# Preparing summed weight tiles in a fixed, lagged order, with the plain copies on ScalarE's DMA queue

## The chip, the cores and the metric

The kernel runs on one core of a Trainium2 chip. Its time is the device time of one execution in microseconds (us); lower is better. The engines are TensorE (PE in the profile, its weight loads PEld), VectorE (DVE), ScalarE (ACT), GpSimd (POOL) and SyncE (SP), each with a queue of its own that it works through in order, and 16 DMA engines that move the data. SP, ScalarE and GpSimd start transfers. A transfer that adds to what is in memory is called an accumulate here; all of them are on GpSimd's queue.

## The reference

A transformer trunk of two layers on 512 tokens of width 1024, in float32. Each layer is an FFN, a mixer with three kinds of attention, and a second FFN:

```
for l in range(DEPTH):
    h = rms_norm(x, norm_g[l, 0])
    x = x + 0.5 * swiglu(h, ffn_w_gate[l, 0], ffn_w_up[l, 0], ffn_w_down[l, 0])
    h = rms_norm(x, norm_g[l, 1])
    ...
    x = x + merged @ w_o[l]
    h = rms_norm(x, norm_g[l, 2])
    x = x + 0.5 * swiglu(h, ffn_w_gate[l, 1], ffn_w_up[l, 1], ffn_w_down[l, 1])
return rms_norm(x, final_g)
```

with `swiglu(h, w_gate, w_up, w_down) = (silu(h @ w_gate) * (h @ w_up)) @ w_down`. The hidden width of the FFN is 2816, 22 tiles of 128. The mixer's branches are neighbourhood attention, differential attention and windowed attention with grouped keys.

## The kernel before

Every product is made of float32 parts: a weight tile is loaded by SP (`weights`, line 90), rounded by ScalarE to its high part (`whi`, line 91), VectorE takes the rest (`wlo`, line 92), and TensorE adds three products (lines 113 to 116). `weights` is called 74 times in a mixer and 24 times in an FFN's down projection (8 output tiles, three pieces each).

The gate and up products of an FFN run for most tiles in class `Seven`: a gate and an up tile of weights form a 2x2 block matrix, and seven products of sums of blocks do the work of eight. For that, sums of weight blocks are needed. In the first FFN they are made as it runs. For the three later FFNs, named (0, 1), (1, 0) and (1, 1) by layer and half, they are prepared ahead in DRAM by `prepare(l, i)`, while earlier work runs. For each of 20 tiles (k = 2 to 21) there are five transfers:

- `d_odd` (line 465): half of the gate and half of the up tile are copied to DRAM by SP's queue; `d_even` (line 466): the gate tile likewise. 512 KB each.
- Three accumulates on GpSimd's queue, all from line 456: the up tile onto `d_odd` (512 KB), half of `d_odd` onto half of `d_even` (256 KB), half of `d_even` onto its other half (256 KB). The second needs the first and both copies, the third needs the second.

`prepare` is a generator. Its step k issues the copies of tile k, the first accumulate of tile k - 2, the second of tile k - 4 and the third of tile k - 6; 26 steps do an FFN. `ahead_by(n)` adds n to what is owed and takes a step for each whole one: `weights` calls it with PACE["mixer"] or PACE["down"], `Seven.tile` with PACE["seven"]. `drained` takes what is left of an FFN's steps before that FFN starts.

What a step issues isn't what stands in the queues: a scheduler orders the instructions of each engine by when it takes their inputs to be ready. `tc.issue_after(loaded[0])` puts what SP issues in a step behind the weight load just issued; nothing fixes the place of the accumulates. Inside `Seven.tile` the method `in_order` chains the instructions of each engine in the order written.

Also on GpSimd's queue stand: the loads `x` and `lg` of the residual (line 62) and its stores `d_x` (line 67); the reciprocal root of a norm (`rs`) and of the differential attention's norm (`rt`), line 177, which TensorE spreads by transposes on line 184; the exchanges `qks` (lines 905, 906); and in neighbourhood attention the bias `nab` (line 1081) and the clearing of `lg` (line 1109), which TensorE transposes on line 1042. The lines 113 to 116, 368 to 371 (down projection), 555 (`Seven`) and 1052 (attention) are TensorE's.

Of the kernel before, what the change touches and what calls it, by code (L numbers as in the profile page):

```python
# [14 lines left out]
ALU = mybir.AluOpType  # L15

P = 128
S = 512
# [11 lines left out]
NA_WIN = (0, 64, 192, 256)  # L30
T5_STEPS = (8, 12, 16, 23, 32, 46, 64, 91)
GBUFS = 2 * MF
PACE = {"mixer": (0.36, 0.3), "seven": {(0, 1): 0.4}, "down": {(0, 0): 0.3, (0, 1): 0.4, (1, 0): 0.25}}
LOW_FIRST = (2, 4, 7)
WIDE, WIDE_FIRST = frozenset((2, 3, 4, 5, 6, 7)), frozenset((3, 4, 5))

# [2 lines left out]
def encoder(ctx: ExitStack, tc: tile.TileContext, a: dict, out: bass.AP):  # L39
# [3 lines left out]
    nc = tc.nc  # L43
# [35 lines left out]


    loaded, lower = [], []
    prepared, ahead, due, owed = {}, [], [], [0.0, 0.0]

    def weights(src, width=1024):
        raw = wpool.tile([P, 1024], F32, tag="raw", name="raw", bufs=3)
        hi = wpool.tile([P, 1024], F32R, tag="whi", name="whi")
        lo = wpool.tile([P, 1024], F32R, tag="wlo", name="wlo")
        for c in range(0, src.shape[-1], width):
            w = slice(c, min(c + width, src.shape[-1]))
            loaded[:] = [nc.sync.dma_start(raw[:, w], src[:, w]).ins]  # L90
            nc.scalar.copy(hi[:, w], raw[:, w])  # L91
            lower[:] = [nc.vector.tensor_tensor(out=lo[:, w], in0=raw[:, w], in1=f(hi[:, w]), op=ALU.subtract).ins]  # L92
        ahead_by(owed[1])
        return hi, lo
# [185 lines left out]
    def ffn(l, i, h, nxt=None):  # L280

        with tc.tile_pool(name="ffn", bufs=1) as fp, ExitStack() as order:
# [71 lines left out]
            if nxt is None:  # L354
                finish(fp, ghi, glo, h, tiles)
                return
            owed[1] = PACE["down"].get((l, i), 0)
            for m in range(KC):
# [87 lines left out]
    def prepare(l, i):  # L446


        prepared[l, i] = {}
        tiles = prepared[l, i]  # L450

        def flat(t):
            return t.rearrange("p n c -> p (n c)")

        def accumulate(out, more):
            nc.gpsimd.dma_start(out, more, accum_op=ALU.add, max_dma_last_dim=4 * 1024)  # L456

        for k in range(2, MF + 6):
            if k < MF:
                gu = a["w_gu"][l, i, k]  # L460
                t31, t24 = [
                    dram.tile([P, 2, S], F32, tag=f"d_{g}{l}{i}_{k}", name=f"d_{g}") for g in ("odd", "even")
                ]
                tiles[k] = t31, t24
                nc.sync.dma_start(t31, gu.rearrange("n p c -> p n c")[:, :, 0:S])
                nc.sync.dma_start(flat(t24), gu[0])
            if k - 2 in tiles:
                accumulate(flat(tiles[k - 2][0]), a["w_gu"][l, i, k - 2, 1])
            if k - 4 in tiles:
                t31, t24 = tiles[k - 4]  # L470
                accumulate(t24[:, 0], t31[:, 1])
            if k - 6 in tiles:
                t24 = tiles[k - 6][1]
                accumulate(t24[:, 1], t24[:, 0])
            yield

    def ahead_by(n):

        owed[0] += n
        while ahead and owed[0] >= 1:  # L480
            owed[0] -= 1
            with tc.issue_after(loaded[0]):
                if next(ahead[0], ahead) is ahead:
                    ahead.pop(0)
                    due.pop(0)

    def drained(l, i):

# [5 lines left out]
    class Seven:  # L494
# [9 lines left out]
        @contextmanager  # L504
        def in_order(self):


            traced = nc.cur_bb.bb.instructions
            last = traced[-1]
            yield  # L510
            start = next(k for k in reversed(range(len(traced))) if traced[k] is last) + 1
            for ins in traced[start:]:
                if ins.engine in self.behind:
                    why = mybir.DependencyInfo(mybir.DependencyClass.NoSync, mybir.DependencyReason.DATA)
                    tc.add_manual_dep(ins, self.behind[ins.engine].name, why, reason="in_order")
                self.behind[ins.engine] = ins

        def fetch(self, m, sums=None):
# [67 lines left out]
        def tile(self, m):  # L586
# [10 lines left out]
            def blocks(w, at=0):  # L597
                return [[t[:, at + k * P : at + k * P + P] for k in range(4)] for t in w]
# [4 lines left out]
            def side(n):  # L603
                return [s.t[n - 1] for s in sides]
# [17 lines left out]
            with self.in_order():  # L622
# [48 lines left out]
                nc.vector.tensor_tensor(out=gn, in0=gn, in1=h.rb, op=ALU.mult)  # L671
                self.product(7, one, blocks(w31), side(3))
            ahead_by(PACE["seven"].get(self.at, 0))
            u3 = self.halves(1, 6, 7)
            hi = fp.tile([P, S], F32R, tag="g", name="g", bufs=GBUFS)
# [702 lines left out]
    def gain(l, i):  # L1378
        return ng[:, (l * 3 + i) * KC : (l * 3 + i + 1) * KC]

    h = Norm(0, gain(0, 0))
    due[:] = [(0, 1), (1, 0), (1, 1)]
    ahead[:] = [prepare(*at) for at in due]
    for l in range(DEPTH):
        n1 = Norm(3 * l + 1, gain(l, 1))
        ffn(l, 0, h, n1)
        n2 = Norm(3 * l + 2, gain(l, 2))
        owed[1] = PACE["mixer"][l]
        mixer(l, n1, n2)
# [94 lines left out]
```

## Time and profile before

| | us |
|---|---|
| median of 3 runs | 2521.67 |
| lowest, highest | 2518.4, 2543.03 |
| the profiled execution, whole | 2516.38 |
| its span, first to last instruction | 2514.5 |
| TensorE idle within the span | 100.6 (2514.5 - 2413.9) |
| mean granted TensorE clock | 0.982 |

The first FFN ends at about 343 us, mixer 0 at 886, the second FFN at 1262, the third at 1618, mixer 1 at 2140. A busy time is that of one engine in the whole span or in a stretch; a wait is time in which an engine stood idle, put down to what released it. The granted clock is the share of its full speed that TensorE was given.

### The profile page before, as it was taken

To read this page: it belongs to the slowest core of one execution; us is meant where nothing else is said; L and a number is where in the kernel's file an instruction comes from. 1 tells how busy PE (TensorE), PEld (TensorE's weight loads), DVE (VectorE), ACT (ScalarE), POOL (GpSimd) and SP (SyncE) were. 2 spreads that over 40 slices of the span, in tenths; PEclk is the share of its full clock that TensorE was granted. 3 is DMA by queue.
4 is the path that set the end of the run, shared out by engine and by line. 5 is a ranking of instruction groups with operands and counts; after the bars stand their busy time and mean duration, and the time that the engine had idled before them with its cause. 6 is when DMAs were issued, how large, how long until landed. Compare 5 with 4: busy or idle time off the path is not lost. (4 is left out here: it accounts for less than half of the span.)

```text
span 2514.5 us, 34878 instructions
## 1 busy us (share of the span) xinstructions
PE 2413.9 (96%) x12762; PEld 2063.4 (82%) x12762; DVE 1722.1 (68%) x3061; ACT 1328.3 (53%) x2433; POOL 349.0 (14%) x524
## 2 busy tenths in 40 slices
PE   9999997898999999999899999988999999999998
PEld 7899876787888888888788888767888888888887
DVE  7998334675766678995379983345667667799932
ACT  6565224664666546663246662246655665566632
POOL 2100213322100011111200002133221000000000
PEclk9999998999999999999999999989999999999999
DMA  6566898676325559899645568866766323455532
GB/s 199 164 182 203 226 276 186 166 202 170 94 89 150 181 178 287 271 276 267 168 157 185 193 200 236 234 166 151 206 171 164 98 84 121 152 196 185 184 115 71
DMA packets 149771, 452.86 MB, mean 180 GB/s; under 512 B 18264, under 2 KB 23688, under 8 KB 148640
## 3 DMA queue, kind: packets, MB, share of 16 engines
q1 hardware_dynamic: 108096, 341.42, 40.1%
q0 software_dynamic: 40352, 107.36, 21.6%
q8 instruction: 100, 1.64, 0.3%
q10 hardware_dynamic: 1152, 1.86, 0.2%
q14 instruction: 71, 0.58, 0.1%
HBM read 428.52 MB, written 138.44 MB: 225 GB/s over the span
## 5 line engine op out<-in xcount | busy, mean ns | idle before, releaser
L91 ACT CAST whi<-raw 128x1024 fp32r<-128x1024 f32 (+1 forms) x258 | 264.6, 1031 | 397.7 <-PE mm L369 149.2
L92 DVE TENSOR_TENSOR wlo<-raw,whi 128x1024 fp32r<-128x1024 f32 (+1 forms) x258 | 321.2, 1246 | 214.5 <-ACT whi L91 120.2
L113 PE MATMUL mm<-h,whi 128*128 128x512 f32 x800 | 321.6, 402 | 0.7 <-ACT h L144 0.7
L114 PE MATMUL mm<-h,whi 128*128 128x512 f32 x800 | 316.2, 395 | 0.0
L368 PE MATMUL mm<-g,whi 128*128 128x512 f32 x528 | 208.0, 394 | 7.5 <-ACT whi L91 7.5
L369 PE MATMUL mm<-g,whi 128*128 128x512 f32 x528 | 207.5, 393 | 0.0
L116 PE MATMUL mm<-h,wlo 128*128 128x512 f32 x800 | 197.7, 389 | 0.0
L100 DVE TENSOR_TENSOR wlo<-raw,whi 128x1024 fp32r<-128x1024 f32 x156 | 184.3, 1219 | 7.8 <-ACT whi L99 7.7
L113 PEld LDWEIGHTS mm<-h,whi 128*128 128x128 f32 x800 | 152.3, 190 | 30.5 <-ACT h L144 1.5
L114 PEld LDWEIGHTS mm<-h,whi 128*128 128x128 f32 x800 | 152.2, 190 | 29.7 <-DVE h L145 0.5
L116 PEld LDWEIGHTS mm<-h,wlo 128*128 128x128 f32 x800 | 150.2, 188 | 31.4
L99 ACT CAST whi<-raw 128x1024 fp32r<-128x1024 f32 x156 | 156.8, 1052 | 16.3 <-DMA raw<-in_w_gu 13.9
L371 PE MATMUL mm<-g,wlo 128*128 128x512 f32 x528 | 131.4, 389 | 0.0
L1011 ACT ACTIVATE lg<-lg,negm 128x256 f32<-128x256 f32 (+1 forms) x192 | 114.1, 595 | 32.2 <-DVE negm L1008 31.0
L368 PEld LDWEIGHTS mm<-g,whi 128*128 128x128 f32 x528 | 100.6, 190 | 29.3 <-ACT whi L91 8.3
L369 PEld LDWEIGHTS mm<-g,whi 128*128 128x128 f32 x528 | 100.4, 190 | 21.0
L371 PEld LDWEIGHTS mm<-g,wlo 128*128 128x128 f32 x528 | 99.1, 188 | 20.6
L681 ACT COPY gu<-mm 128x512 f32<-128x512 f32 (+1 forms) x78 | 41.9, 537 | 126.7 <-PE mm L555 126.7
L456 POOL DMA_DIRECT2D d_even<-d_odd x60 | 50.4, 840 | 381.9 <-DMA d_odd<-in_w_gu 342.5
L607 DVE TENSOR_TENSOR gu<-pr,gu 128x256 f32<-128x256 f32 x234 | 98.3, 420 | 6.4 <-ACT gu L640 3.8
L1253 DVE TENSOR_TENSOR z<-mm,rb 128x512 f32<-128x512 f32 x48 | 33.2, 691 | 97.4 <-PE mm L116 97.4
L892 DVE SCALAR_TENSOR_TENSOR qn<-mm,rb 128x512 f32<-128x512 f32 x44 | 34.8, 795 | 94.7 <-PE mm L116 68.6
(312 smaller groups left out, 5920.9 us busy)
## 6 DMA issues: line engine op xcount, KB each, us to landing
raw<-in_w_gu SPq DMA_DIRECT2D x94, 512.0 KB, 4.2
d_odd<-in_w_gu SPq DMA_DIRECT2D x60, 512.0 KB, 6.4
d_even<-in_w_gu SPq DMA_DIRECT2D x60, 512.0 KB, 7.1
d_odd<-in_w_gu POOLq DMA_DIRECT2D x60, 512.0 KB, 7.4
wsum<-d_odd SPq DMA_DIRECT2D x60, 512.0 KB, 3.3
raw<-d_even SPq DMA_DIRECT2D x60, 512.0 KB, 4.5
raw<-in_w_down SPq DMA_DIRECT2D x48, 512.0 KB, 5.1
raw<-in_w_gate SPq DMA_DIRECT2D x48, 512.0 KB, 3.9
```

The costliest lines, as they stand in the source:

```text
L91: nc.scalar.copy(hi[:, w], raw[:, w])
L92: lower[:] = [nc.vector.tensor_tensor(out=lo[:, w], in0=raw[:, w], in1=f(hi[:, w]), op=ALU.subtract).ins]
L99: nc.scalar.copy(hi, src)
L100: nc.vector.tensor_tensor(out=lo, in0=src, in1=f(hi), op=ALU.subtract)
L113: nc.tensor.matmul(ps, wh, xhi[k], start=k == 0, stop=False)
L114: nc.tensor.matmul(ps, wh, xlo[k], start=False, stop=False)
L116: nc.tensor.matmul(ps, wl, xhi[k], start=False, stop=k == n - 1)
L368: nc.tensor.matmul(ps, w[k][0], ghi[c + k], start=c + k == 0, stop=False)
L369: nc.tensor.matmul(ps, w[k][0], glo[c + k], start=False, stop=False)
L371: nc.tensor.matmul(ps, w[k][1], ghi[c + k], start=False, stop=c + k == MF - 1)
L607: nc.vector.tensor_tensor(out=out, in0=in0, in1=in1, op=ALU.add)
L1011: nc.scalar.activation(p, p, AF.Exp, bias=negm, scale=-1.0, accum_out=total)
```

## The change

The two copies of a step are issued by ScalarE instead of SP. `queued` pins each of the five transfers behind the instruction traced last on its engine, and behind the preparing transfer issued last on that engine; these edges order the issue and wait for nothing. `issue_after(loaded[0])` is gone from `ahead_by`. The pace in mixer 0 goes from 0.36 to 0.42 steps a weight load and in the Seven loop of FFN (0, 1) from 0.4 to 0.25 a tile. The edge's description, made in place before, has the name `NO_WAIT`.

```diff
-PACE = {"mixer": (0.36, 0.3), "seven": {(0, 1): 0.4}, "down": {(0, 0): 0.3, (0, 1): 0.4, (1, 0): 0.25}}
+NO_WAIT = mybir.DependencyInfo(mybir.DependencyClass.NoSync, mybir.DependencyReason.DATA)
+PACE = {"mixer": (0.42, 0.3), "seven": {(0, 1): 0.25}, "down": {(0, 0): 0.3, (0, 1): 0.4, (1, 0): 0.25}}
...
-    prepared, ahead, due, owed = {}, [], [], [0.0, 0.0]
+    prepared, ahead, due, owed, queue = {}, [], [], [0.0, 0.0], {}
...
+        def queued(dma):
+
+            tc.keep_in_program_order(dma)
+            engine = dma.ins.engine
+            if engine in queue:
+                tc.add_manual_dep(dma.ins, queue[engine], NO_WAIT, reason="queued")
+            queue[engine] = dma.ins.name
+
         def accumulate(out, more):
-            nc.gpsimd.dma_start(out, more, accum_op=ALU.add, max_dma_last_dim=4 * 1024)
+            queued(nc.gpsimd.dma_start(out, more, accum_op=ALU.add, max_dma_last_dim=4 * 1024))
...
-                nc.sync.dma_start(t31, gu.rearrange("n p c -> p n c")[:, :, 0:S])
-                nc.sync.dma_start(flat(t24), gu[0])
+                queued(nc.scalar.dma_start(t31, gu.rearrange("n p c -> p n c")[:, :, 0:S]))
+                queued(nc.scalar.dma_start(flat(t24), gu[0]))
...
-            with tc.issue_after(loaded[0]):
-                if next(ahead[0], ahead) is ahead:
-                    ahead.pop(0)
-                    due.pop(0)
+            if next(ahead[0], ahead) is ahead:
+                ahead.pop(0)
+                due.pop(0)
```

The rows below are the instructions of one engine in the order in which the built kernel has them; a number behind a tile's name tells one buffer from another, so that equal numbers are the same tile. In the changed kernel line 456 is 465, 465 and 466 are 474 and 475, 177 is 178, 67 is 68, 1109 is 1116, 905 and 906 are 912 and 913, and 91 is 92.

GpSimd, end of the first down projection and start of mixer 0, around the norm's root `rs`, before:

```order
L67 DMA d_x_3473<-x_3468 128x512
L456 DMA d_even_3707<-d_odd_3706 128x512
L456 DMA d_even_3707<-d_even_3707 128x512
L456 DMA d_odd_3803<-in_w_gu 128x1024
L67 DMA d_x_3577<-x_3572 128x512
L456 DMA d_even_3804<-d_odd_3803 128x512
L177 TENSOR_TENSOR rs_3627<-rt_3628,nhalf_80 128x4
L456 DMA d_even_3804<-d_even_3804 128x512
```

and now:

```order
L68 DMA d_x_3473<-x_3468 128x512
L465 DMA d_odd_3286<-in_w_gu 128x1024
L465 DMA d_even_3083<-d_odd_3082 128x512
L465 DMA d_even_2875<-d_even_2875 128x512
L68 DMA d_x_3577<-x_3572 128x512
L178 TENSOR_TENSOR rs_3627<-rt_3628,nhalf_80 128x4
L465 DMA d_odd_3395<-in_w_gu 128x1024
L465 DMA d_even_3185<-d_odd_3184 128x512
L465 DMA d_even_2976<-d_even_2976 128x512
```

Before, the three accumulates of one tile follow each other, each reading what the last one writes; now three that stand together belong to three tiles.

GpSimd in the neighbourhood attention of mixer 0, around two clears of `lg`, before:

```order
L456 DMA d_odd_4878<-in_w_gu 128x1024
L906 DMA qks_4441<-qk_4435 64x512
L905 DMA qks_4441<-qk_4435 64x512
L905 DMA qks_4444<-qk_4438 64x512
L906 DMA qks_4444<-qk_4438 64x512
L1109 MEMSET lg_4475 128x2x64
L1109 MEMSET lg_4536 128x2x64
L456 DMA d_even_4879<-d_odd_4878 128x512
L456 DMA d_even_4879<-d_even_4879 128x512
```

and now:

```order
L1116 MEMSET lg_4482 128x2x64
L465 DMA d_odd_4119<-in_w_gu 128x1024
L913 DMA qks_4448<-qk_4442 64x512
L912 DMA qks_4448<-qk_4442 64x512
L912 DMA qks_4451<-qk_4445 64x512
L913 DMA qks_4451<-qk_4445 64x512
L465 DMA d_even_3774<-d_odd_3773 128x512
L465 DMA d_even_3499<-d_even_3499 128x512
L1116 MEMSET lg_4543 128x2x64
```

The first clear now stands ahead of the trio and the exchanges, the second behind all of them.

ScalarE in the first down projection, between two residual tiles (`h` scales one, `gu` takes its squares), before:

```order
L91 CAST whi<-raw 128x1024
L91 CAST whi<-raw 128x768
L91 CAST whi<-raw 128x1024
L144 ACTIVATE h_3167<-x,ng 128x512
L155 ACTIVATE gu<-x 128x512
```

and now:

```order
L92 CAST whi<-raw 128x1024
L474 DMA d_odd<-in_w_gu 256x1x512
L475 DMA d_even<-in_w_gu 16x8192
L92 CAST whi<-raw 128x768
L92 CAST whi<-raw 128x1024
L145 ACTIVATE h_3167<-x,ng 128x512
L156 ACTIVATE gu<-x 128x512
```

The pair of copies stands behind a weight cast and ahead of the next ones; on SP's queue only the loads are left there.

More of the change, by code (lines that the diff above doesn't have):

```diff
@@ L513, in in_order @@
                 if ins.engine in self.behind:
-                    why = mybir.DependencyInfo(mybir.DependencyClass.NoSync, mybir.DependencyReason.DATA)
-                    tc.add_manual_dep(ins, self.behind[ins.engine].name, why, reason="in_order")
+                    tc.add_manual_dep(ins, self.behind[ins.engine].name, NO_WAIT, reason="in_order")
                 self.behind[ins.engine] = ins
```

## The prediction

> **What bounds the kernel now.** I read the page first, then the list of what TensorE waited for, the table of stretches, GpSimd's waits and its timeline. The page's span and busy line:
>
> ```profile
> span 2514.5 us, 34878 instructions
> PE 2413.9 (96%) x12762; PEld 2063.4 (82%) x12762; DVE 1722.1 (68%) x3061; ACT 1328.3 (53%) x2433; POOL 349.0 (14%) x524
> ```
>
> TensorE is the bound; only the 100 us in which it is idle, and the time in which it runs slowly, can be won. TensorE's waits (engine, tile, line <- what released it: us in total, times, longest):
>
> ```profile
> PE st L184 <- POOL rs L177: 25.1, 2, 16.8
> PE t L1042 <- POOL lg L1109: 23.6, 5, 8.6
> PE st L184 <- POOL rt L177: 11.4, 2, 9.5
> PE mm L368 <- ACT whi L91: 7.5, 2, 4.6
> PE mm L555 <- ACT gu L634: 7.1, 7, 4.0
> ```
>
> The first, second and third name GpSimd, an engine busy for 14% of the span: 25.1 + 23.6 + 11.4 = 60.1 us. The table of stretches (us, then each engine's busy time and count, granted clock, DMA share, GB/s) says where: the first stretch below is the first down projection, the second the start of mixer 0, the third the part of mixer 1 after the last prepared tile.
>
> ```profile
> 235.00:343.00 108.00, 108.00 (x497) 90.20 (x496) 46.26 (x58) 32.97 (x43) 20.67 (x28) 1.00 0.91 255
> 343.00:400.00 57.00, 39.47 (x168) 31.87 (x167) 18.52 (x21) 12.49 (x16) 17.00 (x23) 0.85 0.79 201
> 1870.00:2140.00 270.00, 268.20 (x1322) 222.94 (x1321) 183.51 (x378) 161.29 (x334) 24.38 (x36) 1.00 0.41 123
> ```
>
> The same mixer code loses 17.5 us in 57 beside the preparation and 1.8 us in 270 without it. GpSimd's own waits say why:
>
> ```profile
> POOL d_even L456 <- DMA d_odd<-in_w_gu: 342.5, 51, 12.7
> POOL d_odd L456 <- DMA d_odd<-in_w_gu: 274.9, 28, 58.7
> POOL d_even L456 <- DMA d_even<-d_odd: 233.7, 53, 8.1
> ```
>
> It stands in its own queue until the transfer just issued has landed, and whatever is queued behind stands with it. GpSimd's timeline where `rs` is late (start, us, instruction, idle before):
>
> ```profile
> 372.97 0.86 POOL L456 DMA_DIRECT2D d_even<-d_odd  x1 [9.21 <-DMA d_odd<-in_w_gu]
> 381.12 0.82 POOL L456 DMA_DIRECT2D d_even<-d_even  x1 [7.29 <-DMA d_even<-d_odd]
> 389.19 0.86 POOL L456 DMA_DIRECT2D d_even<-d_odd  x1 [5.83 <-issue]
> 389.75 1.37 POOL L177 TENSOR_TENSOR rs<-rt,nhalf 128x4 f32<-128x4 f32 x1
> ```
>
> VectorE's and TensorE's timelines of that place, and then the same hand-over before the third FFN, where GpSimd was free:
>
> ```profile
> 369.93 0.15 DVE L176 TENSOR_SCALAR rt<-st 128x4 f32<-128x4 f32 x1
> 372.42 1.98 PE L116 MATMUL mm<-h,wlo 128*128 128x512 f32 x8
> 391.18 1.12 PE L184 MATMUL st<-ident,rs 128*128 128x128 f32 x4 [16.79 <-POOL rs L177]
> ...
> 1286.64 0.16 DVE L176 TENSOR_SCALAR rt<-st 128x4 f32<-128x4 f32 x1
> 1286.88 1.20 POOL L177 TENSOR_TENSOR rs<-rt,nhalf 128x4 f32<-128x4 f32 x1 [7.16 <-DVE rt L176]
> ```
>
> At 370.08 the input of `rs` was there; TensorE had work until 374.4. A free GpSimd would start 0.1 us later, as at 1286.88, and be done near 371.5: the whole 16.79 us goes.
>
> **The change, part by part.**
>
> Order of the accumulates. All 180 stay, but none follows the transfer it needs: in the rows of order above, each reads what was issued one or two steps earlier. A step comes after 1/0.3 weight loads in the first down projection (24 loads in 108 us: 15 us a step), more than a landing (the waits above are 12.7 us at most). So `rs` and `rt` come in time: +36.5 us, bounds 18 (half) and 36.5.
>
> The `lg` clears. They are behind the trio too, and TensorE follows at once:
>
> ```profile
> 482.68 0.81 POOL L456 DMA_DIRECT2D d_odd<-in_w_gu  x1 [8.43 <-DMA d_odd<-in_w_gu]
> 485.50 0.47 POOL L1109 MEMSET lg<- 128x128 f32 x2
> 485.89 0.90 PE L1042 MATMUL t<-ident,lg 128*128 128x128 f32 x3 [6.88 <-POOL lg L1109]
> ```
>
> Here I don't take all. Before has one place where lagged accumulates were issued with nothing to wait for, the drain before the second FFN:
>
> ```profile
> 927.83 0.96 POOL L456 DMA_DIRECT2D d_odd<-in_w_gu  x1
> 929.01 1.50 POOL L456 DMA_DIRECT2D d_even<-d_even  x1
> 935.13 0.81 POOL L456 DMA_DIRECT2D d_odd<-in_w_gu  x1 [4.62 <-issue]
> ```
>
> Three go out 0.6 us apart, the fourth waits 4.6 us for nothing that the profile shows: I read it as room in GpSimd's own queue. Before, a clear stood behind one trio of 15 to 20 us; now it stands behind one or two lagged trios, of which the second may wait about 5 us. I take 70% of 23.6: +16.5 us, bounds 0 and 23.6.
>
> The second FFN's down projection. The two waits for `whi` (7.5 us) start at GpSimd too: the casts are queued on ScalarE behind `h`, that waits for `x`, and `x` for its load from GpSimd's queue. VectorE's wait in 1200 to 1260 us:
>
> ```profile
> DVE x L276 <- DMA x<-d_x: 41.8, 3, 20.2
> ```
>
> Lagged trios let the load through: +7.5 us, bounds 0 and 7.5.
>
> The clock after a stall. TensorE's timeline at one of these two waits; ahead of it eight matmuls take 1.97 us, so a start every (1.97 - 0.39)/7 = 0.226 us:
>
> ```profile
> 1208.16 1.97 PE L371 MATMUL mm<-g,wlo 128*128 128x512 f32 x8
> 1214.78 0.79 PE L368 MATMUL mm<-g,whi 128*128 128x512 f32 x1 [4.64 <-ACT whi L91]
> ...
> 1219.21 0.42 PE L368 MATMUL mm<-g,whi 128*128 128x512 f32 x1
> ```
>
> From 1214.78 to 1219.21 ten matmuls start in 4.43 us instead of 2.26: 2.2 us lost after the stall. Long stalls by the rows above: 16.8 and 8.3 (`rs`), 9.5 (`rt`), 4.6 and 2.9 (`whi`), and of the five for `lg` I count three; five whole and 70% of three are 7.1 x 2.2 = 15.6, taken as +15 us, bounds 8 and 17.6.
>
> The copies on another queue. One late load in the second FFN, ScalarE's and TensorE's timelines:
>
> ```profile
> 965.62 1.99 ACT L99 CAST whi<-raw 128x1024 fp32r<-128x1024 f32 x2 [4.74 <-DMA raw<-in_w_gu]
> 968.45 2.08 PE L555 MATMUL mm<-pair,whi 128*128 128x512 f32 x4 [3.97 <-ACT gu L634]
> ```
>
> The drain of the trios ended there, and SP's queue held copies. With the second gone and the first done in mixer 0, I take +2 us, bounds 0 and 4. The Trainium skill, page "DMA: Bandwidth & Descriptors", section "Issuing engines are not separate DMA queues", speaks against it: whoever starts a transfer, it runs on the same 16 engines among the others, and a second issuer saves only the time of issuing. By that rule this term would be 0 and the time 2 us more; no row here has such copies on ScalarE's queue.
>
> ScalarE now issues 60 pairs. On SP, and for two loads on ScalarE (durations min/median/max, ns):
>
> ```profile
> L465 SPq DMA_DIRECT2D d_odd<-in_w_gu x60: 547/558/1356, 235.1 to 1937.5; - x60
> L466 SPq DMA_DIRECT2D d_even<-in_w_gu x60: 512/607/812, 235.8 to 1938.1; - x60
> L721 ACTq DMA_DIRECT2D raw<-in_w_gu x2: 364/409/454, 1.3 to 1.7; - x2
> ```
>
> 60 x (0.558 + 0.607) = 70 us on an engine busy 53%. Behind a pair wait the next weight cast and, in attention, the exponentials and `ph` casts, and for these TensorE. The cover is ScalarE's idle 47%; if it is gone, a pair costs its 1.2 us. I take a tenth of 70: -7 us, bounds 0 and -35 (half of all pairs in full). SP is relieved of the 70 us; SP is on no row of TensorE's waits, so that is worth nothing beyond the 2 us above.
>
> Pace. Mixer 0 has 74 weight loads: 74 x 0.42 = 31 steps for 27. The Seven loop of the second FFN has 20 tiles: 5 steps for 8. A step moves 2 MB (two copies of 512 KB, accumulates of 512, 256 and 256 KB): 9 MB more in the 545 us of mixer 0 are 16 GB/s on a mean of 180. Nothing, because the first down projection ran at 255 GB/s and a DMA share of 0.91 with TensorE busy 108.00 of 108; if that cover is gone, see the second rival. The name `NO_WAIT` costs nothing.
>
> Sum: 36.5 + 16.5 + 7.5 + 15 + 2 - 7 = 70.5 us off. The profiled execution took 2516.4 us (span 2514.5), which gives 2446. The lowest run shown is 2518.4, 2 us above the profiled one, the median 5: I add 2 and forecast 2448.
>
> **Rivals.**
>
> GpSimd stays the wait. The scheduler packs up to four steps together on GpSimd in the diff attention, and a full queue, as at 935.13, could hold `rt` and `lg` as the landings did. For it: the 4.62. Against: `rs` has only one trio ahead. Half of 60.1 (30), of 7.5 (4) and of the clock (8), and -15 for ScalarE: 27 off, 2491.
>
> The DMA engines become the bound. Mixer 0 gets shorter and has more steps; weight loads come late, as at 965.62. Such a load costs 4 + 2.2 us. From 343 to 620 us about 14 steps lie; if half of them have one, 7 x 6.2 = 43 of the 70 are given back: 2491 again. Against it: the 0.91 with no idle.
>
> Slower: ScalarE's queue blocks. If a copy's issue has to wait, for room or for an earlier transfer, every weight cast behind it waits. Price 60 pairs x the time held on TensorE's path; it decides at 70/60 = 1.2 us a pair (with my 7 us of it in the sum, 1.3). At 2 us: 120 - 77 = 43 slower, 2561. For it: an issue on SP took up to 1356 ns. Against it: the medians, and that a copy waits for no data.
>
> That the order isn't kept would be a rival, but the rows of order show it kept.
>
> **How the numbers follow.** The forecast 0.62, still faster than its bounds 0.04, GpSimd 0.17, DMA 0.11, ScalarE 0.06. The forecast's bounds: all terms at their best are 36.5 + 23.6 + 7.5 + 17.6 + 4 = 89, 2429; the two middle rivals reach 2491. The range 2427 to 2493 takes the forecast and about half of these two. A measurement of this kernel can tell about 1% from no change, 25 us: under 2496.5 is faster. The forecast, what is beyond it and six tenths of the middle rivals are 0.83 faster; the rest of these 0.11 the same; 0.06 slower.
>
> **What would show it.** In the profile of the changed kernel GpSimd's waits of `d_even` for `d_odd` fall from 342.5 to under 60 us; the three GpSimd rows of TensorE's waits from 60.1 to under 15; the stretch at the start of mixer 0 runs at clock 1.00 with under 3 us idle; 60 pairs on ScalarE's queue at medians near 0.56 and 0.61 us. Wrong would be: `rt` or `lg` from GpSimd over 25 us; TensorE waiting for `whi` or `raw` over 30 us in mixer 0; issues on ScalarE of several us.

## The result and the profile after

The changed kernel takes 2423.73 us (median of 4 runs, 2423.16 to 2428.77), the kernel before 2521.98 (4 runs, 2518.4 to 2543.03): a ratio of 0.960 with a 95% interval of 0.954 to 0.965. The direction came as forecast; the gain is larger than forecast, 98 us by the medians instead of 74, and the time lies 3 us below the range. The profiled execution took 2423.72 us. Its span and busy line on the page:

```profile
span 2421.9 us, 34919 instructions
PE 2393.2 (99%) x12762; PEld 2049.1 (85%) x12762; DVE 1709.7 (71%) x3061; ACT 1330.8 (55%) x2433; POOL 361.1 (15%) x524
```

TensorE is now idle for 28.7 us (2421.9 - 2393.2) instead of 100.6, and busy for 20.7 us less with the same 12762 matmuls. These two are the whole gain of the span: 71.9 + 20.7 = 92.6 us. What TensorE still waits for (engine, tile, line <- releaser: us in total, times, longest):

```profile
PE mm L562 <- ACT gu L641: 6.0, 8, 2.8
PE mm L562 <- DVE wlo L101: 3.1, 4, 0.9
...
PE st L185 <- POOL rs L178: 0.3, 1, 0.3
...
PE av L1059 <- DVE pl L1052: 0.2, 1, 0.2
```

The three rows of GpSimd, 60.1 us before, are down to 0.3; those of `rt`, `lg` and of `whi` in the second FFN's down projection are gone. The last row is one that the prediction did not speak of. Before, it was

```profile
PE av L1052 <- DVE pl L1045: 4.8, 5, 1.8
```

GpSimd's own waits in the changed kernel:

```profile
POOL d_odd L465 <- DMA d_odd<-in_w_gu: 237.7, 10, 37.9
POOL d_even L465 <- issue: 56.5, 43, 5.3
POOL d_odd L465 <- issue: 48.0, 18, 6.4
...
POOL d_even L465 <- DMA d_even<-d_odd: 5.4, 2, 3.6
```

The 342.5 and 233.7 us for which `d_even` waited for the accumulate ahead of it are down to 5.4. Two kinds of standing are left. Ten times the first accumulate waits for a copy; four of these waits, of 33 to 38 us, are in the gate and up loop of the second FFN, where TensorE waits for nothing from GpSimd. And 61 times, 104.5 us in all, GpSimd pauses before an accumulate for nothing that the profile shows.

The hand-over at the start of mixer 0, GpSimd's and TensorE's timelines (start, us, instruction, idle before):

```profile
367.88 1.05 POOL L178 TENSOR_TENSOR rs<-rt,nhalf 128x4 f32<-128x4 f32 x1 [4.40 <-DVE rt L177]
368.90 0.89 POOL L465 DMA_DIRECT2D d_odd<-in_w_gu  x1
369.51 1.16 POOL L465 DMA_DIRECT2D d_even<-d_odd  x1
370.05 1.49 POOL L465 DMA_DIRECT2D d_even<-d_even  x1
...
371.96 0.27 PE L185 MATMUL st<-ident,rs 128*128 128x128 f32 x1
```

GpSimd is idle when VectorE hands it `rt`, makes `rs`, and issues the next trio (the three accumulates of a step) within 3 us, without waiting for any of the three to land. The table of stretches from 343 us on, where TensorE had been idle for 17.5 us of 57 before (length, then each engine's busy time and count, clock, DMA share, GB/s):

```profile
343.00:382.00 39.00, 39.00 (x178) 31.70 (x177) 18.17 (x22) 12.84 (x17) 15.03 (x18) 1.00 0.92 254
382.00:420.00 38.00, 37.22 (x180) 30.96 (x179) 21.19 (x50) 23.04 (x50) 13.25 (x22) 1.00 1.04 276
```

The DMA engines are full in the second stretch (the profile's count comes to 1.04), and TensorE loses 0.8 us in both together. The rows of the two copies on ScalarE's queue (durations min/median/max in ns, first and last start):

```profile
L474 ACTq DMA_DIRECT2D d_odd<-in_w_gu x60: 548/548/668, 238.9 to 1843.4; - x60
L475 ACTq DMA_DIRECT2D d_even<-in_w_gu x60: 519/628/1305, 241.0 to 1844.0; - x60
```

Sixty pairs at 0.55 and 0.63 us, as they were on SP's queue.

**Where the clock went.** The table of stretches before, just after the stall of 16.79 us that ended at 391.18:

```profile
390.00:392.00 2.00, 0.82 (x5) 0.82 (x5) 0.00 (x0) 0.00 (x0) 1.12 (x2) 0.50 0.60 41
392.00:394.00 2.00, 2.00 (x7) 1.61 (x6) 1.05 (x2) 0.91 (x2) 0.17 (x1) 0.50 0.50 90
394.00:396.00 2.00, 2.00 (x7) 1.52 (x6) 1.91 (x2) 0.92 (x2) 2.00 (x4) 0.50 0.42 41
396.00:398.00 2.00, 2.00 (x9) 1.65 (x8) 1.97 (x2) 0.00 (x0) 2.00 (x5) 0.84 0.50 90
```

TensorE is back at work but is granted half its clock for 5 us more. I cut the whole span into such stretches of 2 us and added up, over all, busy time x (1 - clock): 21.5 us before, 2.6 after. Before, there are ten such troughs with work in them, 2.1 us each at the mean: after the two stalls for `rs` (378 and 1632 us), that for `rt` (600), three for `lg` (482, 1680, 1734), two for `whi` (1212, 1250), the late load (966), and one near 100 us in the first FFN. Only the last is left in the changed kernel. That is 18.9 of the 20.7 us of busy time.

### The profile page after: what moved, and what is told of

Read it like the earlier page. It is cut to its first block, busy times and chain, and to the rows that moved or that the text cites. A ratio compares the mean times of both kernels' runs of the same rounds, so it can differ in the third digit from the quotient of the medians.

```text
span 2421.9 us, 34919 instructions
## 1 busy us (share of the span) xinstructions
PE 2393.2 (99%) x12762; PEld 2049.1 (85%) x12762; DVE 1709.7 (71%) x3061; ACT 1330.8 (55%) x2433; POOL 361.1 (15%) x524
## 3 DMA queue, kind: packets, MB, share of 16 engines
q0 software_dynamic: 40352, 107.36, 22.1%
## 4 chain that ended last, share of the span: by engine, by line
PE 90%; DVE 4%; issue 2%; ACT 1%; DMA 1%; POOL 1%; SPq 0%; POOLq 0%; ACTq 0%; DVEq 0%
PE mm L562 17%; PE pr L562 8%; PE mm L117 8%; PE mm L115 8%; PE mm L114 8%; PE mm L369 5%; PE mm L372 5%; PE mm L370 5%; PE pv L562 4%; PE mm L1277 2%; PE av L1059 2%; PE mm L1273 2%; PE mm L1272 2%; PE t L1049 1%; PE s L1004 1%
## 5 line engine op out<-in xcount | busy, mean ns | idle before, releaser
L93 DVE TENSOR_TENSOR wlo<-raw,whi 128x1024 fp32r<-128x1024 f32 (+1 forms) x258 | 310.4, 1203 | 233.3 <-ACT whi L92 118.6
L465 POOL DMA_DIRECT2D d_odd<-in_w_gu x60 | 52.1, 868 | 294.9 <-DMA d_odd<-in_w_gu 237.7
L100 ACT CAST whi<-wsum 128x1024 fp32r<-128x1024 f32 x78 | 82.1, 1053 | 24.2 <-PE pv L562 24.2
L101 DVE TENSOR_TENSOR wlo<-wsum,whi 128x1024 fp32r<-128x1024 f32 x78 | 94.8, 1215 | 0.0
```

The lines of the kernel that those rows point to most:

```text
L100: nc.scalar.copy(hi, src)
L101: nc.vector.tensor_tensor(out=lo, in0=src, in1=f(hi), op=ALU.subtract)
```

## The experiments

Times are medians; "idle" is the span less TensorE's busy time, "low clock" the sum just described, "rest" the span less both; these three are of the one profiled execution of each kernel. The ratios are to runs of the kernel before on the same chip.

| kernel | us | ratio, interval | idle | low clock | rest |
|---|---|---|---|---|---|
| before | 2521.98 | | 100.6 | 21.5 | 2392.4 |
| the change | 2423.73 | 0.960, 0.954 to 0.965 | 28.7 | 2.6 | 2390.6 |
| order alone | 2420.65 | 0.962, 0.958 to 0.965 | 25.1 | 4.7 | 2389.4 |
| queue alone | 2497.19 | 0.991, 0.988 to 0.995 | 83.7 | 24.1 | 2388.3 |
| pace alone | 2487.69 | 0.988, 0.984 to 0.992 | 84.7 | 11.0 | 2390.5 |
| order and pace, SP's queue | 2423.02 | 0.962, 0.959 to 0.966 | 27.4 | 2.7 | 2388.9 |
| order and queue, old pace | 2423.78 | 0.963, 0.961 to 0.965 | 29.4 | 7.3 | 2386.1 |
| pinned without lag | 2490.41 | 0.989, 0.988 to 0.991 | 77.9 | 22.7 | 2389.4 |
| lag of one step | 2424.53 | 0.963, 0.960 to 0.966 | 31.0 | 4.7 | 2388.7 |
| copies in halves | 2424.40 | 0.963, 0.961 to 0.965 | 28.3 | 5.5 | 2389.6 |
| root held, 4 more | 2438.42 | 0.970, 0.965 to 0.975 | 41.1 | 10.1 | 2389.7 |
| root held, 8 more | 2470.64 | 0.982, 0.979 to 0.985 | 66.5 | 9.4 | 2389.8 |
| root held, 16 more | 2527.80 | 1.003, 1.002 to 1.004 | 120.3 | 17.9 | 2387.9 |
| no accumulates | 2413.85 | 0.959, 0.957 to 0.961 | 22.1 | 2.4 | 2387.8 |

The rest is the same within 6.3 us in all fourteen, so idle time and low clock account for nearly all that these kernels differ by.

**Order alone.** The pins on the accumulates are put into the kernel before; its queue and pace stay.

```diff
-            nc.gpsimd.dma_start(out, more, accum_op=ALU.add, max_dma_last_dim=4 * 1024)
+            queued(nc.gpsimd.dma_start(out, more, accum_op=ALU.add, max_dma_last_dim=4 * 1024))
```

> The kernel before with one part of the change: the accumulates on GpSimd's queue are pinned in the lagged order; the copies stay on SP's queue behind the weight loads and the pace is the old one. Theory A (the lagged order of the accumulates carries the gain, because GpSimd no longer stands in its queue until a transfer has landed): TensorE's waits for rs, rt and lg fall from 60 to under 10 us, its busy time falls by about 20 us as the clock stays up, and the time is 2424 to 2445 us. Theory B (the lagged order only moves the wait: copies and weight loads on SP's queue come late instead, and it takes the free queue of ScalarE to have the gain): waits for rs, rt and lg fall, waits for whi or raw grow to 20 us and more, 2455 to 2495 us.

Measured 2420.65 us. No row of TensorE's waits names `rs`, `rt` or `lg` from GpSimd; its first rows are

```profile
PE mm L563 <- ACT gu L642: 5.2, 5, 2.4
PE mm L563 <- DVE wlo L101: 2.9, 4, 0.9
```

Theory A, in a time 3 us under its range: the order of the accumulates carries the whole gain, and the late loads of theory B did not come.

**Queue alone.** The copies go to ScalarE's queue (one of the two is shown), and `issue_after` is gone; the accumulates are not pinned, the pace is the old one. The copies themselves keep their pins on ScalarE's queue, so "without any pinned order" below holds for the accumulates alone.

```diff
-                nc.sync.dma_start(flat(t24), gu[0])
+                queued(nc.scalar.dma_start(flat(t24), gu[0]))
```

> The kernel before with the copies issued by ScalarE, without any pinned order and with the old pace. Theory A: the accumulates of one tile still follow each other, GpSimd still stands for each landing, and TensorE's waits for rs, rt and lg stay at 40 to 80 us: 2505 to 2535 us. Theory B (the queue counts): the copies land sooner, the accumulates wait less and the loads come in time: 2455 to 2495 us.

Measured 2497.19 us: 0.9% faster, between the two ranges. Of B one part came: the copies land about 1 us sooner at the median (5.1 and 6.2 us after their issue instead of 6.4 and 7.1). The accumulates do not wait less; GpSimd stands as before, in its own waits and in TensorE's:

```profile
POOL d_even L465 <- DMA d_odd<-in_w_gu: 358.9, 53, 10.2
...
PE st L185 <- POOL rs L178: 18.1, 2, 13.4
PE t L1049 <- POOL lg L1116: 12.0, 2, 6.1
PE st L185 <- POOL rt L178: 10.6, 3, 9.3
```

The trios stand for landings just as long (358.9 us instead of 342.5), and TensorE still waits 40.7 us for GpSimd. Its span is 18.4 us less than before. TensorE waits less for `lg` (12.0 us instead of 23.6) and for `rs` (18.1 instead of 25.1), and 9.4 us more for an `h` from ScalarE. Why it is caught less by the standing GpSimd stays open.

**Pace alone.** Only the two numbers change.

```diff
-PACE = {"mixer": (0.36, 0.3), "seven": {(0, 1): 0.4}, "down": {(0, 0): 0.3, (0, 1): 0.4, (1, 0): 0.25}}
+PACE = {"mixer": (0.42, 0.3), "seven": {(0, 1): 0.25}, "down": {(0, 0): 0.3, (0, 1): 0.4, (1, 0): 0.25}}
```

> The kernel before with the two numbers of the pace changed and nothing else. Theory A (the pace counts for nothing by itself; it puts four more steps into mixer 0, where the stalls are): 2510 to 2540 us, TensorE's waits for rs, rt and lg 50 to 80 us. Theory C (the pace carries part of the gain by taking three steps out of the gate and up loop of the second FFN): 2485 to 2510 us.

Measured 2487.69 us, 1.2% faster: A is wrong here, and C holds for the larger part. TensorE's longest waits in the second FFN (886 to 1262 us) before:

```profile
PE mm L368 <- ACT whi L91: 7.5, 2, 4.6
PE mm L555 <- ACT gu L634: 4.1, 2, 4.0
```

and the longest there with this pace:

```profile
PE mm L555 <- DVE wlo L100: 0.9, 1, 0.9
```

The waits for `whi` and the late load, 11.6 us together, are gone but for 0.2, and with them three troughs of the clock (2.2, 1.7 and 2.5 us): 18 of the 28.3 us by which its span is shorter. The stalls for GpSimd in the mixers stay, 55.2 us in the whole span instead of 60.1:

```profile
PE st L184 <- POOL rs L177: 31.0, 2, 20.2
PE t L1042 <- POOL lg L1109: 18.7, 3, 11.1
PE st L184 <- POOL rt L177: 5.5, 2, 4.5
```

**Order and pace on SP's queue; order and queue with the old pace.** With the order alone and the whole change these make a square of queue and pace under the fixed order. The first edit is shown for one of the two copies; `issue_after` is back in it as well.

```diff
-                queued(nc.scalar.dma_start(flat(t24), gu[0]))
+                nc.sync.dma_start(flat(t24), gu[0])
```

```diff
-PACE = {"mixer": (0.42, 0.3), "seven": {(0, 1): 0.25}
+PACE = {"mixer": (0.36, 0.3), "seven": {(0, 1): 0.4}
```

> The changed kernel with the copies put back on SP's queue, behind the weight load just issued, as before. Theory A (ScalarE's queue brings nothing and costs nothing): 2420 to 2432 us, all of the gain. Theory A' (ScalarE's 70 us of issuing cost something, as the forecast had it with 7 us): 2410 to 2420 us, faster than the changed kernel. Theory B (the queue brings part of the gain): 2440 us and more, with waits for whi, raw or gu from late loads.

> The changed kernel with the old pace. With the order alone, the order with the new pace on SP's queue, and the whole change, it is the fourth of a square of queue and pace under the fixed order. If neither counts under the fixed order: 2419 to 2428 us. If the new pace is needed with ScalarE's queue: 2432 us and more, with waits in the gate and up loop of the second FFN.

Measured 2423.02 and 2423.78 us. The four corners are 2420.65, 2423.02, 2423.73 and 2423.78: with the order fixed, neither queue nor pace counts for more than some 3 us, which these runs can't tell from nothing. None of the other parts beats the order alone, and neither does their sum.

**Pinned without lag.** The pins stay, but a step issues all three accumulates of one tile.

```diff
-            if k - 4 in tiles:
-                t31, t24 = tiles[k - 4]
+            if k - 2 in tiles:
+                t31, t24 = tiles[k - 2]
...
-            if k - 6 in tiles:
-                t24 = tiles[k - 6][1]
+            if k - 2 in tiles:
+                t24 = tiles[k - 2][1]
```

> The changed kernel with all pins kept, but without the lag: a step issues the three accumulates of one tile (that of two steps before) one behind the other. Theory A (what helps is that no accumulate follows the one whose result it needs): GpSimd stands for landings again, TensorE's waits for rs, rt and lg are 30 to 80 us, 2475 to 2530 us. Theory D (what helps is the fixed place of the accumulates, away from rs, rt and lg; the lag adds nothing): these waits stay under 10 us, 2415 to 2440 us.

Measured 2490.41 us, as theory A and not D. GpSimd's wait for its own transfer and TensorE's waits are back:

```profile
POOL d_even L465 <- DMA d_odd<-in_w_gu: 342.7, 55, 11.5
...
PE st L185 <- POOL rs L178: 18.2, 3, 7.3
PE t L1049 <- POOL lg L1116: 17.5, 2, 13.7
PE t L1144 <- DVE lg L1205: 10.8, 2, 5.5
```

GpSimd stands as long as the 342.5 us of before. So a fixed place alone is not what helps: the lag is. The lag alone does not help either: the text of the kernel before has it too, and without the pins the scheduler undid it.

**Lag of one step.** Tiles k - 1, k - 2 and k - 3 instead of k - 2, k - 4 and k - 6.

> The changed kernel with half the lag: each accumulate is one step behind the transfer that it needs, not two. Theory A1 (a step in the mixers comes after some 18 us and in a down projection after some 15 us, a landing takes 8 us at the median: one step is enough): 2420 to 2432 us, GpSimd's waits of d_even for d_odd under 60 us. Theory A2 (where the scheduler lets two or more steps follow each other closely, as at the start of the differential attention, one step is too little): 2435 to 2475 us, waits for rs, rt or lg of 10 to 40 us.

Measured 2424.53 us, as theory A1; GpSimd's waits of `d_even` for what it reads are 18.9 us. One wait for `rs` of 2.3 us and one for `lg` of 2.2 us have come back.

**Copies in halves.** Each copy on ScalarE is issued as two of half the size (one of the two copies is shown).

```diff
-                queued(nc.scalar.dma_start(flat(t24), gu[0]))
+                for n in range(2):
+                    queued(nc.scalar.dma_start(flat(t24)[:, n * S : n * S + S], gu[0][:, n * S : n * S + S]))
```

> The changed kernel with each copy on ScalarE issued as two halves: 240 issues instead of 120, the same bytes (a half of the d_even copy goes in rows of 2 KB), so some 70 us more of issuing on ScalarE. The forecast's step (a tenth of ScalarE's issuing lies on TensorE's path): 7 us more, 2429 to 2433 us. Rival (none of it does; ScalarE's idle 45% covers it): 2421 to 2426 us. If instead half of it lay on the path: 2455 us and more.

Measured 2424.40 us, with TensorE idle for 28.3 us instead of 28.7. A half takes nearly as long to issue as a whole copy, 0.51 and 0.61 us at the median, so the issuing did double. It costs nothing that can be seen: the forecast's tenth is wrong, the rival holds.

**Root held.** Line 178 repeats at the six roots `rs` of the norms.

```diff
-        root = nc.gpsimd.tensor_tensor(out=rs[:, :4], in0=rt[:, :4], in1=nhalf[:, :4], op=ALU.pow)
+        for _ in range(hold + 1):
+            root = nc.gpsimd.tensor_tensor(out=rs[:, :4], in0=rt[:, :4], in1=nhalf[:, :4], op=ALU.pow)
```

> The changed kernel with GpSimd held before the six roots rs of the norms: line 178 is executed 9 times instead of once with the same result, about 9 us more each. It measures what a wait of TensorE costs beside its length. Theory C (the granted clock falls during a stall of more than about 4 us and comes back some 5 us after TensorE resumes, whatever the stall's length): TensorE's busy time grows by about 2.1 us for each root that it waits for, and as much in the kernel held 16 times; 2424 + its waits + 2.1 each, about 2424 + 4 x (6 + 2) to 6 x (9 + 2): 2455 to 2490. Theory E (the time at low clock grows with the stall): the growth in busy time with 16 is twice that with 8.

> The same with line 178 executed 17 times at the six roots rs, about 19 us more each. Theory C: waits of TensorE some 10 us longer at each root than with 8, busy time grown by the same 2.1 us a root as with 8; 2510 to 2555 us. Theory E: busy time grown by about 4 us a root.

> The changed kernel with line 178 executed 5 times at the six roots rs, for short waits. With 8 more the six waits were 3.7 to 11.9 us, and 16 more made them 8 to 12 us longer, so about 1 us for each: with 4 more, waits of some 5, 2.5, 8, 0.5, 2.5 and 0 us, 18 us in all. Theory F (a wait under about 2.5 us leaves the clock alone, a longer one costs 1.5 to 2 us more): two to four troughs of the granted clock at these roots, 4 to 8 us lost in them, 2443 to 2452 us. Theory G (every wait of a microsecond or more costs a trough): five troughs, 8 us or more.

Measured 2438.42, 2470.64 and 2527.80 us. TensorE's waits for `rs` with 4 more:

```profile
PE st L186 <- POOL rs L179: 16.3, 4, 7.2
```

with 8 more:

```profile
PE st L186 <- POOL rs L179: 42.2, 6, 11.9
```

and with 16 more:

```profile
PE st L186 <- POOL rs L179: 96.0, 6, 18.7
```

Each wait has one trough behind it: 7.6 us in four with 4 more (1.9 each), 9.4 in six with 8 (1.6), 15.6 in six with 16 (2.6). The wait at the mean goes from 4.1 to 7.0 and 16 us. The times with 8 and 16 are in C's ranges, but the cost of a trough is not fixed, as C had it: it lies between 1.4 and 3.0 us. Nor does it follow the wait, as E had it: it is smaller with 8 than with 4 more. The busy time did grow twice as much with 16 as with 8, 12.6 us and 6.0, as E said; but the trough near 100 us is missing with 8, and at the roots themselves the troughs add up to 1.7 times as much, for waits 2.3 times as long. With one profile each, what sets the cost stays open. Theory F's four troughs came (in a time 5 us under its range), but its limit of 2.5 us is wrong. G's five did not come, as only four roots waited; a longer wait without a trough stands in the last section. One of the two shortest waits with 4 more, in TensorE's timeline:

```profile
381.52 1.11 PE L186 MATMUL st<-ident,rs 128*128 128x128 f32 x4 [2.24 <-POOL rs L179]
```

and the stretches behind it:

```profile
382.00:384.00 2.00, 2.00 (x7) 1.71 (x7) 0.71 (x2) 0.59 (x1) 2.00 (x5) 0.50 0.53 78
384.00:386.00 2.00, 2.00 (x8) 1.60 (x8) 1.91 (x2) 1.24 (x2) 2.00 (x5) 0.81 0.99 190
```

**No accumulates.**

> The changed kernel without the 180 accumulates: the sums are not formed, the copies alone are made. It bounds what the accumulates still cost, on GpSimd's queue and on the DMA engines. Theory A (nothing is left of it on TensorE's path): 2414 to 2424 us. Rival (late transfers among the loads still cost something): 2395 to 2413 us, TensorE's idle time falling from 29 us to under 15.

Measured 2413.85 us, a hair under what theory A allowed and above what the rival did. Idle time falls by 6.6 us, not to under 15. By the medians the accumulates still cost 10 us; 6.6 of them are idle time, and the rest is within the 6.3 us by which these accounts differ anyway. Another order of the accumulates could hardly win more than that.

## Where the prediction held, and which of its sizes failed

Against the profiled execution's span (2514.5 to 2421.9, 92.6 us):

| term | forecast | measured | from |
|---|---|---|---|
| `rs` and `rt` | +36.5 | +36.2 | TensorE's waits; 0.3 left |
| `lg` clears | +16.5 | +23.6 | no row of `lg` from GpSimd is left |
| `whi` in the second FFN's down projection | +7.5 | +7.5 | no row is left |
| clock | +15 | +20.7 | TensorE's busy time |
| late load, copies on the other queue | +2 | +1.1 | `gu`, 7.1 to 6.0 |
| ScalarE's issuing | -7 | 0 | copies in halves |
| `pl` and the other small waits | not in the sum | +3.5 | what is left of 71.9 |
| sum | +70.5 | +92.6 | |

The mechanism held, and the sum was 22.1 us short. Three steps were mis-sized and make 19.8 us of it: the `lg` clears (16.5 instead of 23.6), ScalarE's issuing (7 us charged, none found) and the clock (15 instead of 20.7). The small waits, put at nothing without a reason, make 3.5 us more.

**What bounds the kernel.** Right. The profile showed an engine busy for 14% of the time as the one waited for, and the run without lag and the order alone show that its standing in its own queue was the reason. One reading was too narrow: "12.7 us at most" passes over the row of 58.7 us, in which the first accumulate waits for a copy. That wait stayed, at up to 37.9 us.

**The `lg` clears: the first step that failed.** "A clear now stands behind one or two lagged trios, of which the second may wait about 5 us", hence 70%. The pause of 4.62 us from which this came is real, and there are 61 of its kind in the changed kernel. Two trios in a row then look as in GpSimd's and TensorE's timelines here:

```profile
379.45 0.88 POOL L465 DMA_DIRECT2D d_odd<-in_w_gu  x1 [1.27 <-issue]
...
391.47 0.81 POOL L465 DMA_DIRECT2D d_odd<-in_w_gu  x1 [6.40 <-issue]
...
396.27 0.81 POOL L465 DMA_DIRECT2D d_even<-d_even  x1 [1.34 <-issue]
...
399.02 0.63 POOL L1116 MEMSET lg<- 128x128 f32 x2
...
406.29 0.71 PE L1049 MATMUL t<-ident,lg 128*128 128x128 f32 x5
```

From the first issue to the last of two trios 17 us pass, as forecast and more, but the clears behind are done 6.6 us before TensorE first wants one. I gave the pause a price without asking when the thing behind it is needed. The cover is not endless: with a lag of one step a clear came 2.2 us late, and with the old pace on ScalarE's queue two came late, 3.5 us in all. The rival "GpSimd stays the wait" falls on the same rows.

**The clock.** The price of a stall was right (2.2 us forecast, 2.1 measured over ten troughs); the count was short. Nine troughs went: the five counted whole, three at `lg` of which the 70% took 2.1, and one behind the late load at 968.45, which the sum priced without its clock. 1.8 us of the 20.7 are not explained by the troughs.

**ScalarE's issuing.** "A tenth of 70" was a guess between 0 and a half, without a row. The issues had just the durations forecast (548 and 628 ns at the median), and ScalarE's idle time covered all of them: twice as many cost nothing. The rival "ScalarE's queue blocks" falls with it; the longest issue took 1305 ns.

**The queue.** The Trainium skill, page "DMA: Bandwidth & Descriptors", section "Issuing engines are not separate DMA queues", says that another issuer saves only the time of issuing. The square of runs agrees: on SP's queue 2420.65 and 2423.02 us, on ScalarE's 2423.78 and 2423.73. My 2 us for it had no ground; the late load that I gave it went with the order alone too, where TensorE's largest wait in the second FFN's loop is 0.9 us. The copies do land about 1 us sooner from ScalarE's queue (5.2 and 6.2 us at the median, 6.2 and 6.9 in the order alone), which the time doesn't show.

**The pace.** Costed at nothing, and nothing it is once the order is fixed. In the kernel before it is worth 1.2% by itself, because it takes the stalls out of the second FFN, a gain that the order has as well: queue, pace and order alone gain 18, 28 and 95 us of span, the three together 92.6.

**The DMA rival.** It falls: at a share of 1.04 between 382 and 420 us TensorE lost 0.8 us.

**Small waits and the offset.** The five waits for `pl` (4.8 us) lie in the neighbourhood attention beside the late clears, and went with them. In the runs this row is 1.9 to 4.8 us in the four kernels whose clears come late by 12 us or more, and 0.2 at most with the lagged order; that they hang on the clears was not tested by itself. The 2 us added for the difference between profiled execution and runs were not there either: the changed kernel's profiled execution (2423.72) is at its median. With the clock at its bound of 17.6 and `pl` left out, the best case of the forecast was 89 us, or 2429; that is why the range ended too early, at 2427.

## What to carry to other kernels

An engine that is busy for a seventh of the time can be what the busiest one waits for: look at what it waits for itself, and let no transfer in its queue depend on the one just issued; one step between them was enough here. Give a delay a price only after asking when the work behind it is needed. Count a stall of TensorE that halves the clock with 2 us more (here 1.4 to 3.1), and remember that partial edits that each help do not add up when they remove the same stalls.

## What the hardware showed that was not expected

- Span less TensorE's idle time less the low-clock sum is 2386 to 2392 us in fourteen kernels that differ by up to 114 us. The granted clock in stretches of 2 us is exact enough for such an account.
- The length of a wait alone does not decide whether the clock falls. A wait of 2.24 us was enough for half the clock afterwards, while a wait of 2.83 us in the changed kernel (for `gu` at 901.75 us) left no trough. The same wait had one with the copies in halves (2.83 us, at 904.42) and with a lag of one step (2.84 us, at 905.26). At the held roots the clock fell 2.1 to 5.3 us after TensorE went idle, an estimate from the mean clock of the stretch in which it fell. The clock came back after some 3 to 6 us of work. The Trainium skill, page "TensorE: Matmul & The Clock Gate", section Part 1 (The HAM clock gate), has the clock halved by an idle window of about 3.4 us and given back after as much work, in a window that runs freely. The halving agrees (0.50), and so does a fall at no fixed point of a wait. The limit does not, going by the wait alone: 2.24 us had a trough.
- GpSimd pauses up to 6.4 us before issuing an accumulate for nothing that the profile shows, 61 times in the changed kernel. What it waits for there stayed open; TensorE's waits for GpSimd are 0.3 us in this kernel.
